# Row tiles 4 to 15 of the input stream loaded by features and normalised by GpSimd and VectorE

## The chip, the cores and the metric

The kernel runs on one core of a Trainium2 chip, as one launch. The metric is the device time of one execution in microseconds (us). Engine names in the profile: PE is TensorE, PEld its weight loads, DVE is VectorE, ACT is ScalarE, POOL is GpSimd, SP is SyncE, which here only issues DMAs.

## The reference, cut to what matters

One transformer-like layer over 256 latent tokens (`x`) and 256 context tokens (`ctx`) of 2048 features, in fp32. Only its opening concerns the change:

```python
shift, scale, gate = split(silu(c) @ w_mod + b_mod, 3)       # and the same from c_ctx
u   = layer_norm(x)   * (1 + scale)   + shift                # mean and variance over the 2048 features
u_c = layer_norm(ctx) * (1 + scale_c) + shift_c
p   = u   @ w_in
p_c = u_c @ w_in[:, :N_KV]
```

Everything behind it (a gated linear recurrence, an attention branch, gates, an output projection) works on `p` and `p_c`.

## The kernel before

The 2048 features are 16 row tiles `kt` of 128. Products want the features on the partitions, so `u` is kept as tiles of 128 features by 2x256 tokens, each split into a high and a low fp32r part; a product is three matmuls, `three` and `three_b` at lines 340 to 348. Weights come as raw fp32 blocks (`raw`, three buffers), are cut into `whi` by ScalarE (L337) and `wlo` by VectorE (L338), two blocks ahead (`LEAD`).

`x` and `ctx` lie in memory with tokens first. `load_rows` (L158) brings them with tokens on the partitions into four tiles `xs`, four row tiles wide each. `ln_stats` (L248) takes mean and variance of each token, so these are one number for each partition, and `normalise` (L258) is one VectorE tensor_scalar with two scalars per partition. `make_x` (L271) normalises four row tiles at a time (8 instructions of 128x512 for row tiles 4 to 11; row tiles 0 to 3 are done by `norm_x` from other places). The tile `xs[3]` has been given back by the time row tiles 12 to 15 are wanted, so `make_x` loads each of them again (L279, 128 partitions x 4 pieces of 512 bytes) into a small rotating buffer (tag T2, 4 buffers) and normalises it with four instructions of 128x128. `make_u` (L284) then transposes the row tile on TensorE, four 128x128 transposes into a PSUM bank (L291); ScalarE applies scale and shift from PSUM (L300) and makes the high part (L302), VectorE the low part (L303).

Scale and shift have to be computed first: the rows of `w_mod` come in 512 KB blocks through a pool of AHEAD = 5 buffers (L187). For row tiles 0 to 3 TensorE multiplies them (L204, 16 blocks), for row tiles 4 to 15 VectorE does (`mod_unit`, L225: two instructions of 128x1024 for each block, four blocks for each row tile). `prep_tasks` (L507) strings these together for one row tile: three units, `make_x`, one unit, `make_u`.

The products over the key and value columns run in the order of VISITS: the chunk, and from which row tile to which, so that products start while later row tiles are being prepared. `weave` and `tick` (L353, L365) put the preparing tasks between the matmuls, evenly by number of matmuls. This order is the one in which the program is written. Each engine's own order is made from it by a scheduler, which may take an instruction earlier that waits for nothing; on the chip each engine then runs its list in order, and so does each queue that issues DMAs.

Of the kernel before, what the change touches and what calls it, by code (L numbers as in the profile page):

```python
# [8 lines left out]
F32 = mybir.dt.float32  # L9
# [3 lines left out]
ALU = mybir.AluOpType  # L13
AX = mybir.AxisListType

P = 128
D = 2048
KT = D // P
# [17 lines left out]
LATE = 13  # L36
GATES = (0,) * 13 + (3, 4, 3, 1, 1, 0, 2, 2)
MOD_PE = 4
AHEAD = 5
DEPTH = 3  # L40
TURN = 5
LEAD = 2
# [8 lines left out]
def block_kernel(ctx: ExitStack, tc: tile.TileContext, a: dict, out: bass.AP):  # L51
    nc = tc.nc
# [12 lines left out]
    def nm(s):  # L65
        uid[0] += 1
        return f"{s}_{uid[0]}"

    def slot(n, dt=F32):
        return big.tile([P, BIG], dt, tag="S8", name=nm(n))  # L70
# [7 lines left out]
    def t2(n):  # L78
        return tp.tile([P, 512], F32, tag="T2", name=nm(n), bufs=4)
# [8 lines left out]
    def aux(n):  # L88
        return ps.tile([P, 512], F32, tag="aux", name=nm(n))
# [3 lines left out]
    def other(n):  # L93

        return (aux if flip[0] else acc)(n)

    mm = nc.tensor.matmul
# [16 lines left out]
    ident = cst[:, C_ID:C_ID + P]  # L114
# [30 lines left out]
    nc.vector.tensor_tensor(c8, c8, sg8, op=ALU.mult)  # L145
    mod_pool = tc.tile_pool(name="mod", bufs=AHEAD)
    mod_open = mod_pool.__enter__()

    def mod_tile():
        if late:  # L150
            return t4("mod")
        return mod_open.tile([P, 1024], F32, tag="mod", name=nm("mod"))

    bst = cp.tile([P, 4, 4, 6], F32, name="bst")
    xg = a["xc"].rearrange("(t p) (g d) -> g p t d", p=P, g=4)
    xs = [slot("xs")[:, :D].rearrange("p (t d) -> p t d", t=4) for _ in range(4)]
# [15 lines left out]
    for r in range(8):  # L172
        pt = aux("scb")
# [10 lines left out]
    def ahead():  # L184
        while stream and len(blocks) < (2 if late else AHEAD):
            t = mod_tile()
            nc.sync.dma_start(t, stream.pop(0))  # L187
            blocks.append(t)
# [47 lines left out]
    def unit_tasks(js, vs):  # L236
        return [(lambda j=j, hf=hf: mod_unit(j, hf, vs), a["w_mod"][j, hf]) for j in js for hf in range(2)]
# [7 lines left out]
    rs0 = cp.tile([P, 4], F32, name="rs0")  # L245
    ag = cp.tile([P, 4, 2], F32, name="ag0")
# [11 lines left out]
    def normalise(x_, t):  # L258
        nc.vector.tensor_scalar(x_, x_, ag[:, t, 0:1], rs0[:, t:t + 1],
                                op0=ALU.subtract, op1=ALU.mult)  # L260
# [3 lines left out]
    def norm_x(kt, n, ts=range(4)):  # L264

        for t in ts:
            normalise(xs[kt // 4][:, t, (kt % 4) * P:(kt % 4 + n) * P], t)

    x_of, normed = {}, {0}

    def make_x(kt):  # L271
        if kt < 12:
            if kt // 4 not in normed:
                normed.add(kt // 4)
                norm_x(kt // 4 * 4, 4)
            xt = xs[kt // 4][:, :, (kt % 4) * P:(kt % 4 + 1) * P]
        else:
            xt = t2("xt")[:, :512].rearrange("p (t d) -> p t d", t=4)
            nc.sync.dma_start(xt, xg[3][:, :, (kt % 4) * P:(kt % 4 + 1) * P])  # L279
            for t in range(4):  # L280
                normalise(xt[:, t, :], t)
        x_of[kt] = xt

    def make_u(kt, seqs=(0, 1)):  # L284
        xt = x_of[kt]
        if kt >= MOD_PE:
            mod_finish(kt, (0, 1))
            mod_finish(16 + kt, (0, 1))
        pt = other("xT")
        for t in (2 * s + i for s in seqs for i in range(2)):  # L290
            nc.tensor.transpose(pt[:, t * P:(t + 1) * P], xt[:, t, :], ident)  # L291
        uf = t2("uf")[:, :512]
        for s in seqs:
            if u[s][kt // 4] is None:
                u[s][kt // 4] = (slot, wslot)[s]("u", F32R)[:, :2048].rearrange(
                    "p (k h t) -> p k h t", k=4, h=2)
            hi = u[s][kt // 4][:, kt % 4, 0, :]
            lo = u[s][kt // 4][:, kt % 4, 1, :]
            f = uf[:, s * 256:(s + 1) * 256]
            nc.scalar.activation(f, pt[:, s * 256:(s + 1) * 256], AF.Identity,  # L300
                                 bias=mv[:, s, kt:kt + 1], scale=mv[:, s, 16 + kt:17 + kt])
            nc.scalar.copy(hi, f)  # L302
            nc.vector.tensor_tensor(lo, f, hi.bitcast(F32), op=ALU.subtract)  # L303
        made.add(kt)


    turn = [0]
# [199 lines left out]
    def prep_tasks(kt):  # L507

        ts = unit_tasks((kt, 16 + kt), (0, 1))
        ts.insert(3, lambda: make_x(kt))  # L510
        return ts + [lambda: make_u(kt)]

    def gate_task(j):
# [3 lines left out]
    for c, k0, k1 in VISITS:  # L517
        _, w, i = chunks[c]
# [9 lines left out]
    between = [[] for _ in VISITS]  # L528
    sums, totals = zip(*(col_tasks(kt) for kt in range(MOD_PE)))
    xu = [(lambda kt=kt: make_x(kt), lambda kt=kt: make_u(kt)) for kt in range(MOD_PE)]  # L530
# [1 line left out]
    tasks.append(totals[0])  # L532
    x_of[0] = xs[0][:, :, 0:P]
    between[1] += sums[1]
    between[2] += [totals[1], xu[1][0], *sums[2][:2], xu[1][1], *sums[2][2:]]
    between[3] += [totals[2], xu[2][0], *sums[3][:1], xu[2][1], *sums[3][1:], lambda: None,
                   totals[3], xu[3][0], lambda: None, xu[3][1]]
    units = [t for kt in range(MOD_PE, KT) for t in prep_tasks(kt)]
# [439 lines left out]
    for c in range(4):  # L978
        i = 8 + (2 * c - 1) * n
# [135 lines left out]
    pt = aux("gr")[:16, :P]  # L1115
# [98 lines left out]
def _swap(w):  # L1214
    return w.reshape(2, 2, 32)[:, ::-1].reshape(HD)


def _layout(i):
    import numpy as np
    w = i["w_in"][0]  # L1220
    cst, rope = _constants()
    qn, kn = i["q_norm_w"][0], i["k_norm_w"][0]
    cw = np.concatenate([i["conv_w"][0], i["conv_b"]], 0)
    xc = np.concatenate([i["x"][0], i["ctx"][0]], 0)
    return {
        "xc": xc,
        "cf": np.stack([i["c"][0], i["c_ctx"]]).reshape(2, KT, P).transpose(2, 1, 0)
        .reshape(P, 32),
        "cc": np.concatenate([i["c"][0], i["c_ctx"]]).reshape(8, 512),
        "w_mod1": i["w_mod"][0].reshape(4, 4, P, 3, KT, P)[:, :, :, :2, :MOD_PE]  # L1230
        .transpose(4, 0, 2, 1, 3, 5).reshape(MOD_PE, 4, P, 1024),
        "w_mod": i["w_mod"][0].T.reshape(48, P, 2, 1024).transpose(0, 2, 1, 3),
        "b_mod": i["b_mod"][0].reshape(48, P).T,
        "w_qa": _blocks(w[:, 0:1024], 512),
        "w_ka": _blocks(w[:, 1024:2048], 512),
        "w_va": _halves(w[:, 2048:4096], 512),
        "w_kv": _halves(w[:, 4096:5152], 352),
        "w_o": _halves(w[:, 5152:7200], 512),
        "w_z": _halves(w[:, 7200:9248], 512),
        "w_qb": _halves(w[:, 9248:11296], 512),  # L1240
        "w_zb": _blocks(w[:, 11296:13344], 512),
        "w_g": _halves(w[:, 13344:17440], 512),
        "w_ba": _halves(i["w_branch_a"][0], 512),
        "w_bb": _halves(i["w_branch_b"][0], 512),
        "w_out": _halves(i["w_out"][0], 512),
        "conv": cw.reshape(4, 16, P).transpose(2, 1, 0),
        "b_if": i["b_if"],
        "mh": i["mh_norm_w"],
        "nw": np.concatenate([qn, _swap(qn), kn, _swap(kn)]).reshape(2, 256),
        "ln": np.concatenate([i["ln_w"], i["ln_b"]], 0),  # L1250
        "cst": cst,
        "rope": rope,
    }
# [18 lines left out]
```

## Time and profile before

| | us |
|---|---|
| median of 3 runs | 1346.44 |
| lowest and highest run | 1344.09, 1348.11 |
| the profiled execution | 1343.62 |
| its span in the trace | 1341.6 |
| TensorE busy in the span | 1296.4 |
| VectorE busy in the span | 976.0 |

The span runs from the first to the last instruction of the program; 2.0 us of the profiled execution lie outside. All times below are counted from the start of the span. A row of the timeline merges neighbouring instructions of one kind: start, time from the first start to the last end, engine, line, operation, output and inputs, shape, count, and in brackets how long the engine had been idle and what ended that. Durations of matmuls overlap, because they are pipelined: their pace is read from start to start.

### The profile page before, as it was taken

The numbers are of one execution on the slowest core, as the hardware profiler recorded it, in microseconds if no ns is written. First come the engines' busy times: TensorE is split into PE (matmuls) and PEld (weight loads), VectorE is DVE, ScalarE is ACT, GpSimd is POOL, SyncE is SP. The second block draws the span as 40 slices with busy tenths as digits, with TensorE's granted clock in tenths as the row PEclk, the third lists the DMA queues.
The fourth block names the chain that finished last, engine by engine and source line by source line (L and its number), as shares of the span: only waits on it lengthen the run. The fifth ranks groups of instructions, "written<-read, shape, count | busy, mean of one in ns | idle before, by whom it ended". The sixth has DMA issues, their size and how long they took to land.

```text
span 1341.6 us, 19662 instructions
## 1 busy us (share of the span) xinstructions
PE 1296.4 (97%) x7541; PEld 1161.7 (87%) x7541; DVE 976.0 (73%) x1577; ACT 649.8 (48%) x928; POOL 54.1 (4%) x83
## 2 busy tenths in 40 slices
PE   6999998999999999999999999999999999999996
PEld 3788988999999988888889999998888888888884
DVE  6698998877986678787787868786555455545667
ACT  4544322324334576676755566565444444434441
POOL 0000000000110011010110000000000000000000
PEclk8999998999999999999999999999999999999999
DMA  9876764885435554555455444445655556576663
GB/s 339 310 260 227 251 221 136 296 306 189 143 111 189 195 167 160 171 181 180 155 162 182 139 161 142 143 139 174 204 198 202 204 197 203 195 275 219 218 219 116
DMA packets 77902, 264.17 MB, mean 197 GB/s; under 512 B 8984, under 2 KB 11688, under 8 KB 77168
## 3 DMA queue, kind: packets, MB, share of 16 engines
q1 hardware_dynamic: 74752, 251.99, 55.5%
q0 software_dynamic: 2448, 10.68, 2.4%
q8 instruction: 59, 0.97, 0.3%
q10 hardware_dynamic: 608, 0.24, 0.1%
q14 instruction: 35, 0.29, 0.1%
HBM read 260.75 MB, written 2.14 MB: 196 GB/s over the span
## 4 chain that ended last, share of the span: by engine, by line
PE 46%; DVE 2%; ACT 1%; DMA 1%; issue 0%; DVEq 0%; ACTq 0%
PE zb L347 2%; PE zb L346 2%; PE zb L348 2%; PE yb L343 2%; PE yb L342 2%; PE yb L341 2%; PE ga L343 2%; PE ga L341 2%; PE ga L342 2%; PE ya L343 2%; PE ya L341 2%; PE ya L342 2%; PE gb L342 2%; PE gb L343 2%; PE gb L341 2%; PE q L342 2%
## 5 line engine op out<-in xcount | busy, mean ns | idle before, releaser
L338 DVE TENSOR_TENSOR wlo<-raw,whi 128x1024 fp32r<-128x1024 f32 (+3 forms) x375 | 445.3, 1190 | 264.5 <-ACT whi L337 259.4
L337 ACT CAST whi<-raw 128x1024 fp32r<-128x1024 f32 (+3 forms) x375 | 380.2, 1016 | 449.2 <-PE p L343 130.8
L342 PE MATMUL p<-wlo,u 128*128 128x512 f32 (+1 forms) x448 | 160.1, 357 | 2.5 <-DVE wlo L338 2.4
L341 PE MATMUL p<-whi,u 128*128 128x512 f32 (+1 forms) x448 | 159.3, 358 | 2.1 <-ACT u L302 1.1
L225 DVE SCALAR_TENSOR_TENSOR junk<-mod,sc 128x1024 bf16<-128x1024 f32 x128 | 153.4, 1221 | 9.4 <-DMA mod<-in_w_mod 9.3
L343 PE MATMUL p<-whi,u 128*128 128x512 f32 (+1 forms) x448 | 159.4, 356 | 0.0
L342 PEld LDWEIGHTS p<-wlo,u 128*128 128x128 f32 x448 | 86.5, 193 | 10.8 <-DVE wlo L338 4.2
L341 PEld LDWEIGHTS p<-whi,u 128*128 128x128 f32 x448 | 85.7, 192 | 11.5 <-ACT u L302 2.5
L343 PEld LDWEIGHTS p<-whi,u 128*128 128x128 f32 x448 | 86.6, 193 | 6.8
L346 PE MATMUL zb<-u,whi 128*128 128x256 f32 x256 | 72.0, 281 | 0.0
L346 PE MATMUL p<-u,whi 128*128 128x256 f32 x256 | 70.6, 278 | 0.7 <-ACT u L302 0.7
L348 PE MATMUL p<-u,wlo 128*128 128x256 f32 x256 | 70.3, 275 | 0.2 <-DVE wlo L338 0.2
L347 PE MATMUL zb<-u,whi 128*128 128x256 f32 x256 | 70.4, 275 | 0.0
L348 PE MATMUL zb<-u,wlo 128*128 128x256 f32 x256 | 70.4, 275 | 0.0
L347 PE MATMUL p<-u,whi 128*128 128x256 f32 x256 | 70.4, 275 | 0.0
L346 PEld LDWEIGHTS p<-u,whi 128*128 128x128 f32 x256 | 48.9, 192 | 2.1 <-ACT u L302 1.2
L341 PE MATMUL z<-whi,u 128*128 128x512 f32 x128 | 49.7, 389 | 0.0
L341 PE MATMUL q<-whi,u 128*128 128x512 f32 x128 | 49.7, 388 | 0.0
L347 PEld LDWEIGHTS p<-u,whi 128*128 128x128 f32 x256 | 49.1, 192 | 0.4 <-issue 0.4
L342 PE MATMUL gb<-wlo,u 128*128 128x512 f32 x128 | 48.7, 381 | 0.8 <-DVE wlo L338 0.8
L342 PE MATMUL z<-wlo,u 128*128 128x512 f32 x128 | 49.2, 384 | 0.2 <-DVE wlo L338 0.2
L348 PEld LDWEIGHTS p<-u,wlo 128*128 128x128 f32 x256 | 49.1, 192 | 0.3 <-DVE wlo L338 0.3
(329 smaller groups left out, 3156.9 us busy)
## 6 DMA issues: line engine op xcount, KB each, us to landing
mod<-in_w_mod SPq DMA_DIRECT2D x96, 512.0 KB, 4.9
raw<-in_w_g SPq DMA_DIRECT2D x64, 512.0 KB, 4.1
raw<-in_w_o SPq DMA_DIRECT2D x32, 512.0 KB, 3.5
raw<-in_w_z SPq DMA_DIRECT2D x32, 512.0 KB, 3.6
raw<-in_w_qb SPq DMA_DIRECT2D x32, 512.0 KB, 3.6
raw<-in_w_zb SPq DMA_DIRECT2D x32, 512.0 KB, 3.4
raw<-in_w_ba SPq DMA_DIRECT2D x32, 512.0 KB, 3.5
raw<-in_w_bb SPq DMA_DIRECT2D x32, 512.0 KB, 4.1
```

The lines of the kernel that those rows point to most:

```text
L225: nc.vector.scalar_tensor_tensor(junk, blk, 1.0, sc[v][:, hf * 1024:(hf + 1) * 1024], op0=ALU.mult, op1=ALU.mult, accum_out=mp[:, v, hf, j ...
L337: nc.scalar.copy(hi, src)
L338: nc.vector.tensor_tensor(lo, src, hi.bitcast(F32), op=ALU.subtract)
L341: mm(o, lhsT=xh, rhs=wh, start=start, stop=False)
L342: mm(o, lhsT=xh, rhs=wl, start=False, stop=False)
L343: mm(o, lhsT=xl, rhs=wh, start=False, stop=stop)
L346: mm(o, lhsT=wh, rhs=xh, start=start, stop=False)
L347: mm(o, lhsT=wh, rhs=xl, start=False, stop=False)
L348: mm(o, lhsT=wl, rhs=xh, start=False, stop=stop)
```

## The change

Row tiles 0 to 3 stay as they are (ROWS = 4). For row tiles 4 to 15 the host hands over a transposed copy `xT`, features first, in blocks of 128 features by 512 tokens (256 KB each). `fetch_x` issues the load of one row tile on SP: row tiles 4 to 11 into the room of `xs[1]` and `xs[2]`, whose tokens-first content was needed for the statistics only; row tiles 12 to 15 into the small rotating buffers. Now the mean and the factor of a token have to be spread along the free axis: `stat_rows`, once, multiplies the broadcast statistics by the identity on TensorE (8 products of 128x128), and ScalarE copies the two PSUM banks to `mr` in SBUF. `make_x` becomes one GpSimd subtraction and one VectorE multiplication of 128x512, and `make_u` has no transposes for these row tiles: ScalarE reads `xt` from SBUF. `mr` takes 4 KB of each partition, as much as one `w_mod` buffer, and AHEAD goes from 5 to 4. `make_x` stands one unit earlier in `prep_tasks`. Row tile 4 is fetched in `stat_rows`, row tiles 5 to 11 each at the end of the `make_u` of the row tile before, row tiles 12 to 15 in `make_x`.

```diff
-AHEAD = 5
+AHEAD = 4
+ROWS = 4
...
+    mr = mod_open.tile([P, 2, 512], F32, name="mr", bufs=1)
...
+    def stat_rows():
+        for i, src in enumerate((ag[:, :, 0], rs0)):
+            pt = other("mr")
+            for t in range(4):
+                mm(pt[:, t * P:(t + 1) * P], lhsT=src[:, t:t + 1].to_broadcast([P, P]), rhs=ident,
+                   start=True, stop=True)
+            nc.scalar.copy(mr[:, i, :], pt)
+        fetch_x(ROWS)
+
+    def fetch_x(kt):
+        if kt < 12:
+            xt = xs[kt // 4].rearrange("p t d -> p (t d)")[:, (kt % 4) * 512:(kt % 4 + 1) * 512]
+        else:
+            xt = t2("xt")[:, :512]
+        nc.sync.dma_start(xt, a["xT"][kt - ROWS])
+        x_of[kt] = xt
 
     def make_x(kt):
-        if kt < 12:
-            if kt // 4 not in normed:
-                normed.add(kt // 4)
-                norm_x(kt // 4 * 4, 4)
-            xt = xs[kt // 4][:, :, (kt % 4) * P:(kt % 4 + 1) * P]
-        else:
-            xt = t2("xt")[:, :512].rearrange("p (t d) -> p t d", t=4)
-            nc.sync.dma_start(xt, xg[3][:, :, (kt % 4) * P:(kt % 4 + 1) * P])
-            for t in range(4):
-                normalise(xt[:, t, :], t)
-        x_of[kt] = xt
+        if kt < ROWS:
+            x_of[kt] = xs[kt // 4][:, :, (kt % 4) * P:(kt % 4 + 1) * P]
+            return
+        if kt not in x_of:
+            fetch_x(kt)
+        xt = x_of[kt]
+        nc.gpsimd.tensor_tensor(xt, xt, mr[:, 0, :], op=ALU.subtract)
+        nc.vector.tensor_tensor(xt, xt, mr[:, 1, :], op=ALU.mult)
...
-        pt = other("xT")
-        for t in (2 * s + i for s in seqs for i in range(2)):
-            nc.tensor.transpose(pt[:, t * P:(t + 1) * P], xt[:, t, :], ident)
+        pt = xt
+        if kt < ROWS:
+            pt = other("xT")
+            for t in (2 * s + i for s in seqs for i in range(2)):
+                nc.tensor.transpose(pt[:, t * P:(t + 1) * P], xt[:, t, :], ident)
...
         made.add(kt)
+        if ROWS <= kt < 11:
+            fetch_x(kt + 1)
...
-        ts.insert(3, lambda: make_x(kt))
+        ts.insert(2, lambda: make_x(kt))
...
-    between[2] += [totals[1], xu[1][0], *sums[2][:2], xu[1][1], *sums[2][2:]]
+    between[2] += [totals[1], xu[1][0], *sums[2][:2], xu[1][1], *sums[2][2:], stat_rows]
...
+        "xT": xc.T.reshape(KT, P, 512)[ROWS:],
```

## Rows read from the trace of the kernel before

**Rows 1.** The page, part 1: busy us, share of the span, instructions.
```profile
PE 1296.4 (97%) x7541; PEld 1161.7 (87%) x7541; DVE 976.0 (73%) x1577; ACT 649.8 (48%) x928; POOL 54.1 (4%) x83
```
**Rows 2.** Busy time by stretch: stretch, length, engines, granted clock, DMA share, GB/s.
```profile
34.00:58.00 24.00, 21.12 (x201) 16.21 (x201) 14.02 (x27) 13.10 (x27) 0.00 (x0) 1.00 0.91 333
58.00:168.00 110.00, 109.56 (x559) 97.63 (x558) 101.81 (x191) 45.37 (x79) 0.15 (x2) 1.00 0.73 246
168.00:201.00 33.00, 32.20 (x153) 27.88 (x152) 32.97 (x64) 8.99 (x14) 0.00 (x0) 1.00 0.70 222
201.00:235.00 34.00, 30.65 (x171) 29.23 (x170) 28.70 (x62) 7.46 (x12) 0.60 (x1) 0.90 0.43 137
235.00:268.00 33.00, 31.85 (x211) 31.02 (x210) 26.48 (x67) 10.82 (x17) 0.00 (x0) 1.00 0.83 297
```
**Rows 3.** Timeline of PE, 57.4 to 59 us: four transposes and the matmuls behind.
```profile
57.50 0.63 PE L291 MATMUL xT<-cst,xs 128*128 128x128 f32 x4
57.89 0.46 PE L341 MATMUL p<-whi,u 128*128 128x512 f32 x1
58.19 0.38 PE L342 MATMUL p<-wlo,u 128*128 128x512 f32 x1
58.41 0.38 PE L343 MATMUL p<-whi,u 128*128 128x512 f32 x1
```
**Rows 4.** One line, L596: fp32 products with 128 columns, the four of `gi`.
```profile
L596 PE MATMUL gi<-cst,gw x8: 272/273/276, 293.0 to 293.8; 128*8 128x128 f32 x8
```
**Rows 5.** Timeline of PE, 47 to 57.9 us: one product of the modulation.
```profile
52.48 0.64 PE L204 MATMUL mod<-mod,cf 128*32 128x256 f32 x8 [0.76 <-DMA mod<-in_w_mod]
```
**Rows 6.** Timeline of SP, the DMA issues, in two stretches.
```profile
44.31 1.15 SPq L187 DMA_DIRECT2D mod<-in_w_mod  x2
...
46.04 4.62 SPq L187 DMA_DIRECT2D mod<-in_w_mod  x4
...
204.56 0.38 SPq L279 DMA_DIRECT2D xt<-in_xc  x1
```
**Rows 7.** DMA issues by line: count, KB each, median us from issue to landing.
```profile
mod<-in_w_mod SPq DMA_DIRECT2D x96, 512.0 KB, 4.9
...
xt<-in_xc SPq DMA_DIRECT2D x4, 256.0 KB, 5.4
```
**Rows 8.** Timeline of POOL from the start: its DMA issue of L565.
```profile
1.31 0.70 POOL L565 DMA_DIRECT2D cst<-in_cst  x1 [0.38 <-issue]
```
**Rows 9.** Groups of DVE by shape, 14 to 33 us and 460 to 620 us.
```profile
L259 DVE TENSOR_SCALAR xs<-xs,ag,rs 128x512 f32<-128x512 f32 x8 | 3.9, 548 | 0.0
...
L883 DVE TENSOR_TENSOR ws<-ws,qT 128x512 f32<-128x512 f32 x5 | 3.4, 686 | 0.0
```
**Rows 10.** Timeline of DVE around row tiles 12 and 14.
```profile
177.28 1.12 DVE L259 TENSOR_SCALAR xt<-xt,ag,rs 128x128 f32<-128x128 f32 x4
178.30 1.23 DVE L338 TENSOR_TENSOR wlo<-raw,whi 128x1024 fp32r<-128x1024 f32 x1
...
210.57 1.12 DVE L259 TENSOR_SCALAR xt<-xt,ag,rs 128x128 f32<-128x128 f32 x4 [1.94 <-DMA xt<-in_xc]
...
212.20 0.89 DVE L338 TENSOR_TENSOR wlo<-raw,whi 128x704 fp32r<-128x704 f32 x1
```
**Rows 11.** Timeline of POOL, 588 to 594 us: two multiplications of 128x512.
```profile
588.74 3.51 POOL L813 TENSOR_TENSOR G<-G,mh 128x512 f32<-128x512 f32 x2 [3.40 <-ACT G L812]
```
**Rows 12.** Timeline of DVE in the same stretch, 588 to 594 us.
```profile
589.63 3.70 DVE L338 TENSOR_TENSOR wlo<-raw,whi 128x1024 fp32r<-128x1024 f32 x2 [0.91 <-ACT whi L337]
```
**Rows 13.** Timeline of PE, 206.9 to 214.3 us, around row tile 14.
```profile
207.98 0.76 PE L341 MATMUL p<-whi,u 128*128 128x352 f32 x4
211.02 1.05 PE L291 MATMUL xT<-cst,xt 128*128 128x128 f32 x4 [2.28 <-DVE xt L259]
213.14 0.66 PE L342 MATMUL p<-wlo,u 128*128 128x352 f32 x1 [1.07 <-DVE wlo L338]
```
**Rows 14.** Busy time by stretch behind that wait, columns as in the second group.
```profile
212.50:219.30 6.80, 6.16 (x21) 6.16 (x22) 5.21 (x12) 0.00 (x0) 0.00 (x0) 0.50 0.33 106
```

More of the change, by code (lines that the diff above doesn't have):

```diff
@@ L267, in norm_x @@
             normalise(xs[kt // 4][:, t, (kt % 4) * P:(kt % 4 + n) * P], t)
-    x_of, normed = {}, {0}
-    def make_x(kt):
-        if kt < 12:
-            if kt // 4 not in normed:
-                normed.add(kt // 4)
-                norm_x(kt // 4 * 4, 4)
-            xt = xs[kt // 4][:, :, (kt % 4) * P:(kt % 4 + 1) * P]
-        else:
-            xt = t2("xt")[:, :512].rearrange("p (t d) -> p t d", t=4)
-            nc.sync.dma_start(xt, xg[3][:, :, (kt % 4) * P:(kt % 4 + 1) * P])
-            for t in range(4):
-                normalise(xt[:, t, :], t)
-        x_of[kt] = xt
+    x_of = {}
+    def stat_rows():
[13 more added lines that the diff above has]
+        x_of[kt] = xt
+    def make_x(kt):
+        if kt < ROWS:
[6 more added lines that the diff above has]
+        nc.vector.tensor_tensor(xt, xt, mr[:, 1, :], op=ALU.mult)
     def make_u(kt, seqs=(0, 1)):
```

## The prediction

> **What bounds the kernel now.** I read the page first, for which engine fills the span; then the busy times by stretch, for what the opening is limited by; then the timelines of single engines at the places the change touches; last the groups of instructions, for prices. The page says TensorE: 97% busy, VectorE 73% [rows 1]. But busy is not pace, and the average hides the opening, which is all the change touches. By stretch it falls into three parts [rows 2]. From 34 to 58 us neither compute engine is full (TensorE 21.1 of 24 us, VectorE 14.0 of 24); there the DMA is at 0.91 of its time, and products wait for `w_mod` blocks: the one at 52.48 had waited 0.76 us for its load [rows 5]. From 58 to 168 us TensorE is full (109.56 of 110) and runs at its pace of 0.22 us from one 512-column matmul to the next [rows 3]; VectorE has 8.2 us left of 110. From 168 to 235 us VectorE is the tight one (32.97 of 33, then 28.70 of 34), TensorE has gaps, and the granted clock falls. The largest gap is at row tile 14: matmuls stop at 208, the transposes wait 2.28 us for the normalised tile, the next matmul waits 1.07 us for a `wlo` [rows 13], and then 6.8 us pass at half clock, 1.2 of 2.4 GHz, with TensorE having just been idle [rows 14]. VectorE had itself stood 1.94 us waiting for the tile's load, with the cut of that `wlo` two places behind [rows 10].
>
> **The change, part by part.** The sum is made against the profiled execution, 1343.6 us, which is 2.8 under the median of the three runs shown, 1346.4. What this measurement can tell from no change is about 0.3%, 4.0 us.
>
> *Transposes.* Four take 0.39 us of TensorE's pace (57.50 to 57.89), and the matmul behind them 0.30 in place of 0.22 [rows 3]. Twelve row tiles lose them: 12 x 0.47 = 5.6 us. Without the slow matmul it would be 12 x 0.39 = 4.7; that is the lower bound. Seven or eight of the twelve lie where TensorE is full, so nothing hides them and the gain is real there, as long as VectorE follows. **-5.6**.
>
> *Statistics along the free axis.* Eight fp32 products of 128 columns. Such a product is two records, and the eight records of `gi` start within 0.8 us, 0.11 apart [rows 4]: 16 x 0.11 = 1.8 us. Cover: TensorE has 2.9 us idle in 34 to 58 [rows 2], but it is idle there because it waits for loads, in order, and the eight come on top. Bounds 0 and 1.8; I take **+1.8**. ScalarE's two copies lie beside other work (13.1 of 24 us busy); so would its reading from SBUF in place of PSUM, which no row prices.
>
> *One `w_mod` buffer less.* A block's load is issued when a buffer comes free. In the busy part of the start the loads leave SP about 1.4 us apart (four within 4.62 us) [rows 6], so each is issued about 1.4 us later; the product at 52.48, already late [rows 5], would be later by that much at worst and not at all where the queue was the limit. Bounds 0 and 1.4, I take the middle: **+0.7**. From 58 to 168 us some eight row tiles are prepared, 14 us each with four blocks, so a block is used every 3.5 us and three blocks ahead are 10 us; landing takes 4.9 [rows 7]: nothing.
>
> *Loads.* Twelve of 256 KB come, four go: 2.1 MB more. At the 333 GB/s of the start that is 6.3 us, if all of it were pushed in front of the `w_mod` blocks. This can happen: the scheduler takes what waits for nothing early, as it took the load of L565, which stands in the program with the gate computations of the middle and was issued at 1.31 us [rows 8]; the eight loads into `xs` wait for the statistics only. From 58 us on the DMA is at 0.73 [rows 2] and has 30 us to spare. Bounds 0 and 6.3; **+0.5**, because from 34 to 58 us the blocks wait for buffers as well as for the queue, and because a row tile early is one that nobody waits for later.
>
> *VectorE's own instructions.* Away: eight of 128x512, together 3.9 us [rows 9], and four groups of 1.12 us for row tiles 12 to 15 [rows 10], 4.5. New: twelve products of 128x512 at 0.69 [rows 9], 8.2. The balance is -0.2: **0**. Where it falls changes: 3.9 us leave the start, up to 5.5 come where VectorE is fuller.
>
> *GpSimd's subtractions.* GpSimd is free (0.15 us busy of 110 [rows 2]). Two multiplications of this size took it 3.51 us, 1.75 each, beside a busy VectorE [rows 11]. They are not free for VectorE: the two cuts it made meanwhile took 3.70 us [rows 12], where one alone takes 1.23 [rows 10], so 1.24 us were lost, 0.62 to each of GpSimd's. Twelve cost VectorE 0 to 7.4 us. The first eight can run early, where VectorE has 10 of 24 us idle. The last four fall in 168 to 235 us: 2.5 us, of which 5.3 us of idle time [rows 2] hides about half: **+1.2**.
> The Trainium skill (GPSIMD Engine Reference, section 8, Key points) says that GpSimd shares its SBUF interfaces with VectorE and contends with VectorE instructions that have two SBUF inputs; the trace agrees, with the 3.70 us above. The page gives no price; if every subtraction shut VectorE out for its whole length the loss would be, as an estimate with the row's 1.75 us, 21 us in place of 7.4, and the row speaks for the smaller.
>
> *New waits.* VectorE's multiplication now waits for GpSimd, which waits for the load. Queued behind it on VectorE are the cuts `wlo` and the modulation units, and TensorE waits for the cuts. For row tiles 4 to 11 the load is out a row tile ahead, those 14 us. For 12 to 15 the load is issued as before and lands after 5.4 us [rows 7]; `make_x` stands one unit earlier, which gives two units, 2 x 2.4 us of VectorE, between it and `make_u`. On SP each added load is one more issue of 0.38 us [rows 6], and SP is idle most of the time. ScalarE's scale and shift, which waited for the transposes, now waits for the multiplication; `whi` copies stand behind it, as before. I take the waits as **0**, with the stall at row tile 14 as it is: TensorE no longer stops at a transpose, but VectorE still stops, and the same `wlo` is behind it.
>
> Sum: -5.6 + 1.8 + 0.7 + 0.5 + 1.2 = -1.4 us, so 1342.2 against the profiled execution and **1345.0** against the median.
>
> **The rivals.**
> *A, the stall at row tile 14 goes.* The wait of 2.28 us was one of the transposes, which are gone, and 1.07 and half of the 6.8 us at half clock came after it: 2.28 + 1.07 + 3.4 = 6.8 us [rows 13, 14]. For it: TensorE has other matmuls to do, and the tile itself is needed much later; and of the four row tiles loaded like this only one stalled, by the accident of where a change of chunk fell. Against it: VectorE's order, which this rival needs changed. 1345.0 - 6.8 = 1338.2.
> *B, VectorE stands behind GpSimd.* Place: row tiles 12 to 15, 168 to 235 us, where VectorE has 0.03 and 5.3 us idle. The tile that was ready at landing is ready 1.75 us later [rows 11]: four times, 7.0 us, and with 2.5 us of contention 9.5, more than the idle 5.3. It decides from the point at which the waits exceed what is idle, that is from three late tiles on. Then TensorE waits for `wlo`, and another stretch at half clock like the one above costs 3.4 us: +7.0 + 3.4, so 1355.4. For it: rows 12 and the 1.94 us that VectorE already waited [rows 10]. Against it: the earlier place of `make_x`.
> *C, the start takes it.* Place: the `w_mod` blocks before 58 us. If the scheduler puts the eight loads in front of them, the 6.3 us come in place of 0.5 and the 1.4 in place of 0.7: +6.5, so 1351.5. It decides from the point at which more than the idle 0.09 x 24 = 2.2 us of DMA are added, that is from three early loads on. Against it: SP's order of issue puts most blocks ahead.
> *D, the transposes were hidden anyway,* because VectorE limits 58 to 168 us as soon as TensorE is faster: its 8.2 idle us shrink by the 5.6 gained. Then -5.6 falls away: 1350.6.
>
> **How the numbers follow.** Forecast 0.36, A 0.35, B 0.18, C 0.08, D 0.03. The likeliest is the forecast, 1345, with a range of its own of 1342 to 1350 (the loads and GpSimd's contention towards their upper ends, the statistics hidden at the lower). Faster by over 0.3% is A: 0.35. Within 0.3% is the forecast: 0.36. Slower is B, C and D, which all lie beyond 4.0 us: 0.29. For 8 in 10 the range goes through A down to 1334 (the stall gone, the statistics and half of the start's costs hidden too) and up through B's middle to 1357; about 0.1 is left out on each side.
>
> **What the profile after would show.** Transposes: 16 left of 64, and each row tile's 14 us becoming 0.5 shorter in 58 to 168 us. Statistics: 16 records of 128 columns before 58 us. Buffers and loads: products L204 that wait for `w_mod` for longer than 0.76 us, and come later than it. GpSimd: twelve subtractions of about 1.75 us, with VectorE's instructions beside them stretched. B would show VectorE idle in front of the multiplication, released by GpSimd, and TensorE behind it waiting for `wlo` in 168 to 235 us; A would show that stretch at full clock. The prediction is wrong if the stretch from 168 to 235 us changes by more than 5 us, or if what stands at 58 us is moved by more than 4.

## The result: 0.6% slower, and the profile after

| | before | after |
|---|---|---|
| median of 7 runs each, us | 1344.09 | 1350.93 |
| lowest and highest run | 1338.55, 1348.11 | 1350.09, 1353.89 |
| the profiled execution (its span) | 1343.62 (1341.6) | 1353.89 (1352.1) |
| ratio to before, 95% interval | | 1.0062 [1.0044, 1.0080] |

The forecast was a small gain, 1345.0 against 1346.4. The change costs 0.6%, 7 us between the medians and 8 by the ratio; the time lies inside the range, on the other side of no change. The profiled execution of after is 3 us above its median.

The difference is made before the gate computations. Their first product (`gc`, L596 before, L619 after) starts 6.65 us later, against 6.84 us between the medians. The two spans differ by 10.5 us, but what lies behind this product took 1063.6 to 1069.7 us in three traces of the kernel before and its variants alone, so the other 3.9 us are within what single executions differ by. Timeline of PE, before and then after (start, duration, engine, line):

```profile
275.85 0.39 PE L596 MATMUL gc<-tri,gw 128*8 128x128 f32 x2
```
```profile
282.50 0.39 PE L619 MATMUL gc<-tri,gw 128*8 128x128 f32 x2
```

Busy time by stretch of after, to be laid beside [rows 2] (length, PE, PEld, DVE, ACT, POOL, granted clock, DMA share, GB/s):

```profile
34.00:58.00 24.00, 22.66 (x206) 17.36 (x198) 12.29 (x22) 14.18 (x31) 1.66 (x5) 1.00 0.86 303
58.00:168.00 110.00, 100.22 (x485) 86.56 (x485) 109.23 (x194) 43.22 (x75) 12.39 (x9) 0.97 0.76 252
201.00:235.00 34.00, 30.26 (x164) 26.84 (x162) 34.00 (x58) 9.83 (x16) 3.33 (x2) 1.00 0.55 180
```

From 58 to 168 us the roles have changed places: before, TensorE was full and VectorE had 8.2 us left; now VectorE is full (109.23 of 110) and TensorE has 9.8 us of gaps. From 201 to 235 us VectorE has no gap at all. The half clock behind row tile 14 [rows 14] is gone: the stretch from 201 to 235 us runs at 1.00.

How far TensorE gets in 58 to 168 us is read from its groups of 512-column products (line, operation, shape, count, busy us, mean ns, idle before). Before, then after:

```profile
L341 PE MATMUL p<-whi,u 128*128 128x512 f32 x137 | 52.3, 383 | 0.0
L342 PE MATMUL p<-wlo,u 128*128 128x512 f32 x136 | 51.8, 381 | 0.4 <-DVE wlo L338 0.4
L343 PE MATMUL p<-whi,u 128*128 128x512 f32 x136 | 51.5, 379 | 0.0
```
```profile
L365 PE MATMUL p<-wlo,u 128*128 128x512 f32 x116 | 45.8, 394 | 5.5 <-DVE wlo L361 5.5
L364 PE MATMUL p<-whi,u 128*128 128x512 f32 x117 | 45.6, 390 | 1.9 <-ACT u L323 1.9
L366 PE MATMUL p<-whi,u 128*128 128x512 f32 x116 | 45.6, 393 | 0.4 <-DVE u L324 0.4
```

409 products before, 349 after: 60 x 0.22 us [rows 3] = 13.2 us behind at 168 us, 2.2 of it brought from the start (the first such product stands at 60.09 in place of 57.89). Behind 168 us after gets about half back, to 6.65, nearly all of it at row tile 14 (table in the section on the prediction's steps). The wait that is new is the one for `wlo`, VectorE's cut of the weights: 0.4 us before, 5.5 (with the 352-column products 6.0) after.

What was added to VectorE's work stands in two timelines side by side. GpSimd's subtractions (L300), and VectorE's instructions at the same times:

```profile
84.54 1.57 POOL L300 TENSOR_TENSOR xs<-xs,mr 128x512 f32<-128x512 f32 x1 [14.30 <-DMA xs<-in_xT]
87.66 1.29 POOL L300 TENSOR_TENSOR xs<-xs,mr 128x512 f32<-128x512 f32 x1 [1.54 <-DMA xs<-in_xT]
101.36 4.43 POOL L300 TENSOR_TENSOR xs<-xs,mr 128x512 f32<-128x512 f32 x2 [6.76 <-DMA xs<-in_xT]
```
```profile
83.75 1.22 DVE L361 TENSOR_TENSOR wlo<-raw,whi 128x1024 fp32r<-128x1024 f32 x1
84.89 2.30 DVE L227 SCALAR_TENSOR_TENSOR junk<-mod,sc 128x1024 bf16<-128x1024 f32 x1
87.73 2.30 DVE L227 SCALAR_TENSOR_TENSOR junk<-mod,sc 128x1024 bf16<-128x1024 f32 x1
...
102.34 2.30 DVE L361 TENSOR_TENSOR wlo<-raw,whi 128x1024 fp32r<-128x1024 f32 x1
104.56 2.30 DVE L227 SCALAR_TENSOR_TENSOR junk<-mod,sc 128x1024 bf16<-128x1024 f32 x1
```

Beside each of these four subtractions one VectorE instruction takes 2.30 us in place of 1.22: 1.08 us more, for a product of the modulation (L227) as for a cut (L361). Of all twelve, ten cost VectorE 1.08 us each, one 0.84, and one nothing, as VectorE stood waiting for its result: 11.6 us.

The rows show how. The two engines take turns. The subtraction of 84.54 ends at 86.11, 1.14 us after the VectorE instruction that was running when it began (83.75 + 1.22 = 84.97). VectorE's next instruction ends 1.08 us after the subtraction (84.89 + 2.30 = 87.19). So it is at all of the lengthened instructions of this size. GpSimd's own rows, 1.27 to 2.27 us, contain its wait for VectorE.

Seven of the twelve subtractions lie in 58 to 168 us. VectorE's multiplications (L301) are there too; its groups in that stretch:

```profile
L227 DVE SCALAR_TENSOR_TENSOR junk<-mod,sc 128x1024 bf16<-128x1024 f32 x60 | 76.6, 1306 | 0.1
...
L301 DVE TENSOR_TENSOR xs<-xs,mr 128x512 f32<-128x512 f32 x7 | 4.7, 677 | 0.0
```

So 7 x 1.08 + 4.7 = 12.3 us were put into a stretch where VectorE had 8.2. This sum is an argument, not a measurement: the experiments show that GpSimd's part of it costs and the multiplications don't.

They lie there because the loads do. Timeline of SP, issues of row tiles 4, 5, 6 and the last of the eight:

```profile
48.82 0.43 SPq L290 DMA_DIRECT2D xs<-in_xT  x1
...
62.46 0.42 SPq L290 DMA_DIRECT2D xs<-in_xT  x1
...
77.53 0.41 SPq L290 DMA_DIRECT2D xs<-in_xT  x1
...
101.68 0.42 SPq L290 DMA_DIRECT2D xs<-in_xT  x1
```

The loads were not taken early to the start: one leaves before 58 us, the others in the order of the program up to 101.68, and each subtraction shown follows its landing.

VectorE's delay costs TensorE more than the waits. Timeline of PE in after:

```profile
112.58 0.48 PE L365 MATMUL p<-wlo,u 128*128 128x512 f32 x1 [2.44 <-DVE wlo L361]
...
117.08 0.48 PE L364 MATMUL p<-whi,u 128*128 128x512 f32 x1 [1.87 <-ACT u L323]
...
119.41 0.63 PE L366 MATMUL p<-whi,u 128*128 128x512 f32 x1
119.84 0.63 PE L364 MATMUL p<-whi,u 128*128 128x512 f32 x1
```

After gaps of 2.44 and 1.87 us the products start 0.43 us apart in place of 0.22, at the lower of the two clocks, for some 3 us; the mean clock of 0.97 in the stretch above is this and a like piece at 61 to 64 us. The second piece is not the subtractions' doing: the run without them, below, has one too (mean clock 0.98).

### The profile page after: what moved, and what is told of

It reads as the page before. It is cut to its first block, busy times and chain, and to the rows that moved or that the text cites. A ratio compares the mean times of both kernels' runs of the same rounds, so it can differ in the third digit from the quotient of the medians.

```text
span 1352.1 us, 19610 instructions
## 1 busy us (share of the span) xinstructions
PE 1295.4 (96%) x7509; PEld 1156.3 (86%) x7509; DVE 985.0 (73%) x1565; ACT 651.4 (48%) x930; POOL 74.9 (6%) x95
## 5 line engine op out<-in xcount | busy, mean ns | idle before, releaser
L361 DVE TENSOR_TENSOR wlo<-raw,whi 128x1024 fp32r<-128x1024 f32 (+3 forms) x375 | 447.7, 1197 | 256.2 <-ACT whi L360 255.8
L227 DVE SCALAR_TENSOR_TENSOR junk<-mod,sc 128x1024 bf16<-128x1024 f32 x128 | 160.5, 1276 | 13.6 <-DMA mod<-in_w_mod 13.4
L364 PE MATMUL ga<-whi,u 128*128 128x512 f32 x128 | 49.4, 386 | 0.0
```

The lines of the kernel that those rows point to most:

```text
L227: nc.vector.scalar_tensor_tensor(junk, blk, 1.0, sc[v][:, hf * 1024:(hf + 1) * 1024], op0=ALU.mult, op1=ALU.mult, accum_out=mp[:, v, hf, j ...
L361: nc.vector.tensor_tensor(lo, src, hi.bitcast(F32), op=ALU.subtract)
L364: mm(o, lhsT=xh, rhs=wh, start=start, stop=False)
```

## The experiments

All times are ratios to runs of the kernel before on the same chip, with the 95% interval in brackets; 0.001 is 1.34 us. Theory 1: GpSimd's subtractions lengthen VectorE's instructions, and VectorE becomes the limit of the opening. Theory 2: the multiplications that VectorE itself got suffice for that. Theory 3: the missing `w_mod` buffer delays the start, and all behind it.

### The buffer alone (theory 3)

The kernel before with one buffer less:

```diff
-AHEAD = 5
+AHEAD = 4
```

> The kernel before with four w_mod buffers in place of five, nothing else. Theory 1 (each GpSimd subtraction shuts VectorE out for 1.08 us, in the stretch from 58 to 168 us where VectorE has 8.2 us idle): no more than 1 us, ratio 0.999 to 1.001. Theory 2 (VectorE's own multiplications, moved from the start into that stretch, are enough): the same. Theory 3 (the missing buffer delays the start): most of the 7 us, ratio 1.003 to 1.005, and the stretch from 34 to 58 us longer.

Measured 1.0012 [0.9986, 1.0037]. The first 512-column product starts at 58.81 in place of 57.89, and the first gate product at 275.40, not later than before. The interval alone still reaches theory 3's 1.003; but all runs of the change below have four buffers too, and one of them is faster than before. Theory 3 is out as the main cause.

### The subtraction on VectorE (theory 2)

The changed kernel without GpSimd:

```diff
-        nc.gpsimd.tensor_tensor(xt, xt, mr[:, 0, :], op=ALU.subtract)
+        nc.vector.tensor_tensor(xt, xt, mr[:, 0, :], op=ALU.subtract)
```

> The changed kernel with the subtraction on VectorE too. VectorE pays 0.6 us for it in place of the 1.08 us that GpSimd's keeps it out. Theory 1: 12 x 0.48 = 5.8 us less VectorE time, so faster than the changed kernel by 2 to 5 us, ratio to before 1.002 to 1.005, and no instruction of 128x1024 over 1.3 us. Theory 2: VectorE has still more of its own, 12 x 0.6 = 7 us, ratio 1.008 to 1.011. Theory 3: no change, 1.006.

Measured 0.9996 [0.9984, 1.0008]. VectorE got twelve more instructions of its own, 12 x 0.69 = 8.2 us, and the kernel is 0.0066, 8.9 us, faster than after. Theory 1 had expected less, 2 to 5 us: VectorE's account is 11.6 - 8.2 = 3.4 us, and 1.2 us for which it had waited for GpSimd. TensorE's mean clock in the stretch below, 1.00 against 0.97, is worth about 3 us more, as an estimate (0.03 of 110 us); no run separates these. The stretch 58 to 168 us:

```profile
58.00:168.00 110.00, 104.86 (x518) 91.40 (x517) 109.83 (x208) 45.60 (x80) 0.15 (x2) 1.00 0.80 267
```

VectorE is as full as in after (109.83), but gets through 208 instructions in place of 194, and TensorE through 518 in place of 485. That busy time is full in both shows that it can't tell the two apart; the counts can. Theory 2 falls.

### No subtraction, and neither subtraction nor multiplication

The changed kernel with the GpSimd line left out, and with both lines left out:

```diff
-        nc.gpsimd.tensor_tensor(xt, xt, mr[:, 0, :], op=ALU.subtract)
```
```diff
-        nc.gpsimd.tensor_tensor(xt, xt, mr[:, 0, :], op=ALU.subtract)
-        nc.vector.tensor_tensor(xt, xt, mr[:, 1, :], op=ALU.mult)
```

> The changed kernel without the subtraction of the mean, so this step of the normalisation is missing. Theory 1: VectorE gets 12 x 1.08 = 13 us back, 7.6 of them from 58 to 168 us, and the kernel is as fast as before or faster, ratio 0.995 to 1.000. Theory 2: the multiplications alone keep it slow, 1.003 to 1.006. Theory 3: no change, 1.006.

> The changed kernel with neither the subtraction nor the multiplication: row tiles 4 to 15 are not normalised. Left are the new loads, the statistics, four w_mod buffers and the missing transposes. Theory 1a (VectorE bounds 58 to 168 us in every form of the change, so each us of its own work counts as much as a us that GpSimd keeps it out): 12 x 0.6 us less than without the subtraction alone, 0.991 to 0.995. Theory 1b (only what GpSimd takes matters; with it gone TensorE bounds again): as without the subtraction, 0.996 to 0.998.

Without the subtraction: 0.9968 [0.9955, 0.9980], 0.0094 or 12.6 us below after, for the 11.6 us by which VectorE's instructions had been lengthened and the 1.2 us of its wait. The first gate product moves from 282.50 to 270.32, 12.2 us. Without both: 0.9984 [0.9971, 0.9998], no further gain: the multiplications, 8.2 us, cost nothing that can be measured, and theory 1a's larger gain of leaving them out didn't come. (The subtractions on VectorE, 8.2 us too, cost 0.0028 or 3.7 us against none.) So a us of VectorE's own work in the opening counts for less than a us of its waiting for GpSimd; why was not settled. Even with neither VectorE is busy for 109.70 of 110 us. The stretch 58 to 168 us without the subtraction, then two stretches without both:

```profile
58.00:168.00 110.00, 106.05 (x521) 93.12 (x518) 109.86 (x208) 45.52 (x79) 0.15 (x2) 0.98 0.83 274
```
```profile
58.00:168.00 110.00, 104.70 (x524) 91.70 (x525) 109.70 (x207) 46.08 (x80) 0.15 (x2) 1.00 0.84 283
201.00:235.00 34.00, 33.80 (x207) 32.35 (x207) 22.09 (x40) 9.80 (x18) 0.60 (x1) 1.00 0.60 196
```

VectorE has 22.09 of 34 us busy in the later stretch (28.70 in [rows 2]): it does in 58 to 168 us what it did later before. From 58 to 168 us TensorE still waits for `wlo` three times, 3.8 us together. Why it has just these gaps wasn't settled.

### The subtractions without the change

The kernel before, with four buffers, and with twelve GpSimd subtractions of 128x512 that read a `w_mod` block and write to a scratch tile that nobody reads:

```diff
+        if MOD_PE <= j < 16 and hf == 1:
+            nc.gpsimd.tensor_tensor(scr[:, 0, :], blk[:, 0:512], scr[:, 1, :], op=ALU.subtract)
```

> The kernel before with four w_mod buffers and twelve GpSimd subtractions of 128x512 whose result nobody needs, one for each row tile from 4 to 15, on a w_mod block. Loads, transposes and VectorE's work are those of before. Theory 1: twelve VectorE instructions beside them take 1.08 us longer; in 58 to 168 us this is 8 x 1.08 = 8.6 us against 8.2 us idle, so 1 to 6 us slower, ratio 1.001 to 1.005. Theory 2: no change against the kernel before with four buffers. Theory 3: what that kernel shows and no more.

Measured 1.0040 [1.0025, 1.0055], first gate product at 281.31 in place of 275.85. None of the change's waits, loads or statistics are there; instructions on an otherwise idle engine, whose results nobody uses, cost 5.4 us, or 3.8 against the run with the buffer alone. This second difference, 0.0028, is just not clear of the noise (about 0.003 either way); by the traces the first gate product is 5.9 us later. They do hold a block's buffer a little longer. The run agrees with theory 1 without the change around it, but not with its place: VectorE's instructions get 8.6 us longer in 58 to 168 us, of which TensorE loses 1.4 us there and 1.9 us more up to 206.

### The subtraction twice, and a second instruction with one input

```diff
         nc.gpsimd.tensor_tensor(xt, xt, mr[:, 0, :], op=ALU.subtract)
+        nc.gpsimd.tensor_tensor(xt, xt, mr[:, 0, :], op=ALU.subtract)
```
```diff
         nc.gpsimd.tensor_tensor(xt, xt, mr[:, 0, :], op=ALU.subtract)
+        nc.gpsimd.tensor_scalar(xt, xt, 0.0, None, op0=ALU.add)
```

> The changed kernel with every GpSimd subtraction done twice, so that the mean is taken off twice and 24 of them run in place of 12. Theory 1 (each one makes one VectorE instruction 1.08 us longer, and VectorE is the limit of the opening): 12 x 1.08 = 13 us more of VectorE, of which 8 to 13 us reach the end: 1.012 to 1.016 of the kernel before. Rival (the changed kernel loses by the chain from load over GpSimd to VectorE, that is by a tile that is ready later): the tiles are loaded a row tile ahead and wait anyway, another 1.5 us is hidden: 1.005 to 1.008, like the changed kernel.

> The changed kernel with a second GpSimd instruction behind each subtraction, one that reads one tensor only (adds the constant 0.0). If VectorE is shut out by any GpSimd instruction of this size, the time is that of the run with the subtraction twice, 1.012 to 1.016. If it is shut out only where GpSimd reads two tensors, VectorE's instructions beside the additions keep their 1.22 us and the time is the changed kernel's, 1.005 to 1.008.

Twice: 1.0143 [1.0115, 1.0171], 0.0081 or 10.9 us above after. VectorE's instructions get 22.1 us longer, 10.5 more than in after, and it waits for GpSimd for 3.7 us in place of 1.2. The time is theory 1's; a chain that hides the second subtraction is out. The stretch 58 to 168 us has VectorE full with fewer instructions again, 182, and the mean clock is down to 0.92:

```profile
58.00:168.00 110.00, 98.86 (x451) 84.99 (x452) 109.64 (x182) 39.04 (x68) 26.69 (x16) 0.92 0.72 234
```

One input: 1.0129 [1.0094, 1.0163]. By the time alone this is the first of the two expectations, that any GpSimd instruction shuts VectorE out alike. The trace says otherwise. Timeline of GpSimd (L301 here is the addition), then of VectorE:

```profile
103.22 1.48 POOL L300 TENSOR_TENSOR xs<-xs,mr 128x512 f32<-128x512 f32 x1 [3.06 <-DMA xs<-in_xT]
104.79 1.54 POOL L301 TENSOR_SCALAR xs<-xs 128x512 f32<-128x512 f32 x1
106.30 1.36 POOL L300 TENSOR_TENSOR xs<-xs,mr 128x512 f32<-128x512 f32 x1
107.75 2.34 POOL L301 TENSOR_SCALAR xs<-xs 128x512 f32<-128x512 f32 x1
```
```profile
96.98 1.23 DVE L233 TENSOR_TENSOR mv<-mp 128x2 f32<-128x2 f32 x1
98.14 0.68 DVE L302 TENSOR_TENSOR xs<-xs,mr 128x512 f32<-128x512 f32 x1
98.74 0.56 DVE L235 TENSOR_TENSOR mv<-mv,bm 128x2 f32<-128x2 f32 x1
99.22 0.15 DVE L233 TENSOR_TENSOR mv<-mp 128x2 f32<-128x2 f32 x1
100.19 0.69 DVE L302 TENSOR_TENSOR xs<-xs,mr 128x512 f32<-128x512 f32 x1 [0.83 <-POOL xs L301]
...
104.91 1.62 DVE L227 SCALAR_TENSOR_TENSOR junk<-mod,sc 128x1024 bf16<-128x1024 f32 x1
...
106.46 2.28 DVE L227 SCALAR_TENSOR_TENSOR junk<-mod,sc 128x1024 bf16<-128x1024 f32 x1
...
108.67 1.62 DVE L362 TENSOR_TENSOR wlo<-raw,whi 128x1024 fp32r<-128x1024 f32 x1
```

Beside a subtraction 1.22 becomes 2.28 to 2.30, beside an addition 1.62: 0.40 us for one input, 1.08 for two. What is added is the same for every length: an instruction of 128x2, 0.15 us, becomes 1.23 beside a subtraction and 0.56 beside an addition. Ten of the twelve additions met a VectorE instruction, 4.0 us; the subtractions cost 10.3 in place of 11.6, as two met VectorE waiting (one in after) and two in part (one in after). This is 2.7 us more of VectorE than in after, but the time grew by 9.0 (1.0129 less 1.0062). The rest fits the other wait that the longer chain on GpSimd made: VectorE waited for GpSimd 0.8 us before 168 us, as the row at 100.19 shows, and 5.8 us in three waits behind it, against 1.2 us in after. That sum, 2.7 + 6.6 - 1.2 = 8.1, is near the 9.0, but no run separates the two; the chain rival, which the run with two subtractions spoke against, has the larger part here.

### Which of the subtractions cost

```diff
-        nc.gpsimd.tensor_tensor(xt, xt, mr[:, 0, :], op=ALU.subtract)
+        (nc.vector if kt < 12 else nc.gpsimd).tensor_tensor(xt, xt, mr[:, 0, :], op=ALU.subtract)
```

and the counterpart with the two engines exchanged.

> The changed kernel with the subtraction on VectorE for row tiles 4 to 11 and on GpSimd for 12 to 15 only. Theory 1 with its place in 58 to 168 us: the seven of after that fell there are gone, so 7 x 1.08 = 7.6 us come back and 8 subtractions of 0.69 us come onto VectorE: close to all on VectorE, 0.999 to 1.003. If the place that costs is 168 to 235 us, as the forecast's rival B had it, nothing comes back: 1.004 to 1.008.

> The counterpart: subtraction on GpSimd for row tiles 4 to 11, on VectorE for 12 to 15. Theory 1 with its place in 58 to 168 us: the loss stays, 1.003 to 1.007. If the place that costs is 168 to 235 us: 0.998 to 1.002.

GpSimd for the last four only: 1.0011 [0.9988, 1.0033]. For the first eight only: 1.0021 [1.0005, 1.0038]. The second is less than was expected: neither place alone makes the loss of after. With the products counted as above, and the first gate product:

| subtraction on GpSimd | 512-column products in 58 to 168 us | first gate product, us | ratio |
|---|---|---|---|
| none (all on VectorE) | 388 | 274.61 | 0.9996 |
| row tiles 12 to 15 | 386 | 275.85 | 1.0011 |
| row tiles 4 to 11 | 352 | 277.21 | 1.0021 |
| all (after) | 349 | 282.50 | 1.0062 |

The first eight cost 36 products, 7.9 us, by 168 us; but if the last four are not on GpSimd, most of it is regained behind 201 us. Part of that is a wait of 2.09 us for a `wlo` at 214 us in the run that it is compared with, all on VectorE. With all twelve on GpSimd less is regained. That VectorE has time there for the one and not for the other is the likely reason, but not shown. The stretch 201 to 235 us, of the last four only and then of the first eight only:

```profile
201.00:235.00 34.00, 33.20 (x194) 31.25 (x193) 33.65 (x64) 10.52 (x19) 4.66 (x3) 1.00 0.58 176
```
```profile
201.00:235.00 34.00, 33.18 (x190) 31.00 (x190) 33.55 (x63) 8.60 (x14) 0.27 (x1) 1.00 0.54 168
```

TensorE gets 194 and 190 products done there, in after 164. The intervals of the two ratios overlap, so the traces, one of each, carry this more than the times do.

### Other places for the work

The new way for row tiles 12 to 15 only (`ROWS = 12`, the rest as before); all eight loads with the statistics ahead of the first products; and, with the subtraction on VectorE, the modulation of row tile 4 given from VectorE to TensorE (`MOD_PE = 5`):

```diff
-ROWS = 4
+ROWS = 12
```
```diff
-        fetch_x(ROWS)
+        for kt in range(ROWS, 12):
+            fetch_x(kt)
...
-    between[2] += [totals[1], xu[1][0], *sums[2][:2], xu[1][1], *sums[2][2:], stat_rows]
+    between[2] += [totals[1], xu[1][0], *sums[2][:2], xu[1][1], *sums[2][2:]]
...
+    stat_rows()
```
```diff
-MOD_PE = 4
+MOD_PE = 5
...
+    between[4] += [*sums[4], totals[4], xu[4][0], lambda: None, xu[4][1]]
```

> The changed kernel with ROWS = 12: only row tiles 12 to 15 go the new way, 4 to 11 are normalised at the start and transposed as before. From 58 to 168 us no GpSimd subtraction is left. Theory 1: that stretch is as in the kernel before, and four subtractions of 1.08 us fall in 168 to 235 us, where VectorE was full to 168 to 201 us only: ratio 0.999 to 1.003. A theory that puts the loss on the statistics or on the missing buffer: 1.004 to 1.006.

> The changed kernel with the statistics spread and all eight loads of row tiles 4 to 11 issued before the first products, so that GpSimd can subtract where VectorE is idle. Theory 1: from 58 to 168 us VectorE's long instructions are gone and TensorE gains 5 to 8 us there; but the eight loads and the multiplications, which VectorE's list has ahead of the cuts, hold up the start by 4 to 12 us: ratio 0.998 to 1.006, with the start of the 512-column matmuls later by that much. If place doesn't matter, 1.006 as the changed kernel with no change at the start.

> The changed kernel with the subtraction on VectorE and the modulation of row tile 4 moved from VectorE to TensorE: VectorE loses eight instructions of 1.22 us, 9.8 us, TensorE gets sixteen products more, 2.3 us. Theory 1 (VectorE bounds 58 to 168 us): faster than with the subtraction on VectorE alone by 4 to 8 us, ratio to before 0.994 to 0.997. If TensorE bounds there: slower by 2, 1.001 to 1.003.

The last four only: 1.0022 [1.0009, 1.0034]. The start loses 3.4 us (61.3 in place of 57.9 for the first 512-column product), and only 0.6 of it is regained by the first gate product: at row tile 14 TensorE waits 3.62 us for a `wlo`, and the stretch 201 to 235 us is at a mean clock of 0.90 again.

All eight early: 1.0030 [1.0018, 1.0043], less than after. This is the place that the prediction had in mind:

```profile
34.00:58.00 24.00, 17.34 (x142) 14.14 (x139) 18.42 (x25) 7.59 (x20) 8.64 (x9) 0.86 0.63 232
```

The subtractions are here now (GpSimd 8.64 us), and from the first 512-column product to the gates it is 212.0 us in place of 222.4 in after; up to the 409th product it loses 1.3 us against before, where after loses 11.0. But the first product stands at 65.8: 7.9 us later than before, TensorE has only 17.34 of 24 us busy. The early place has a price too.

Row tile 4 on TensorE: 1.0039 [1.0019, 1.0059], a miss; a gain was expected. Its stretches:

```profile
58.00:66.00 8.00, 6.30 (x36) 3.99 (x36) 7.61 (x15) 3.25 (x9) 0.00 (x0) 0.79 0.86 296
66.00:74.00 8.00, 8.00 (x52) 5.23 (x51) 5.19 (x9) 1.73 (x5) 0.00 (x0) 1.00 0.97 356
```

VectorE is freed from 66 us on (5.19 of 8 us), but before that TensorE waits 2.0 us for one of its blocks and runs at a mean clock of 0.79, and then the DMA is at 0.97 of its time. TensorE has 360 of the 512-column products done by 168 us in place of 388.

No kernel that computes the whole was faster than before.

## Why the prediction was wrong, by its steps

**The step that failed is GpSimd's subtractions, +1.2 us.** Measured: 8.9 us against doing them on VectorE, 12.6 us against leaving them out. It failed twice.
- *Price.* 0.62 us each, against 1.08. The two cuts of [rows 12] had lost 1.24 us, and this was shared out between the two GpSimd multiplications of [rows 11]. One by one, the same rows of before say something else. GpSimd, then VectorE:

```profile
588.74 1.29 POOL L813 TENSOR_TENSOR G<-G,mh 128x512 f32<-128x512 f32 x1 [3.40 <-ACT G L812]
590.17 2.08 POOL L813 TENSOR_TENSOR G<-G,mh 128x512 f32<-128x512 f32 x1
```
```profile
589.63 1.48 DVE L338 TENSOR_TENSOR wlo<-raw,whi 128x1024 fp32r<-128x1024 f32 x1 [0.91 <-ACT whi L337]
591.06 2.27 DVE L338 TENSOR_TENSOR wlo<-raw,whi 128x1024 fp32r<-128x1024 f32 x1
```

  The first multiplication ran for the most part while VectorE was idle, and cost the first cut 0.25 us. The second met VectorE at work and cost 1.04, near the 1.08 of after. The 1.75 us of the estimate "for its whole length" were too long, since the 2.08 contain GpSimd's wait for the first cut; its idea, that VectorE waits until GpSimd has done, was right. The cost to VectorE, 11.6 us, is outside the bounds of 0 to 7.4 and below the 21.
- *Place.* The first eight were to run in 34 to 58 us. One did, at 52.90. The premise was the load of [rows 8], which the scheduler had taken early; these loads it issued in program order. So seven fell into the stretch that the prediction itself had found with 8.2 us of VectorE left, with 4.7 us of multiplications beside them. The prediction says that up to 5.5 us come "where VectorE is fuller", and then books the balance of the whole kernel, zero, in place of that of the stretch. By the stretch's balance either alone would have fitted into 8.2 us and the sum, 12.3, would not; a warning, though not a measure, as the multiplications turned out to cost nothing.

**The rest of the sum came near by luck.** Without that term it is -5.6 + 1.8 + 0.7 + 0.5 = -2.6 us. The run without the subtraction gives 0.9968, -4.3 us [-6.0, -2.7]. But the gain is not where the sum has it. The table has by how much later than before TensorE begins the same product (minus: earlier):

| us | 1st product of 512 columns | 241st | 409th | in front of row tile 14 | behind it | first gate product |
|---|---|---|---|---|---|---|
| before, at | 57.9 | 111.7 | 168.0 | 206.2 | 221.0 | 275.8 |
| after | 2.2 | 13.0 | 13.2 | 14.2 | 7.8 | 6.6 |
| all on VectorE | 1.5 | 3.8 | 4.5 | 3.3 | -0.3 | -1.2 |
| no subtraction | 1.7 | 3.1 | 4.3 | 3.4 | -3.8 | -5.5 |
| before, with subtractions | 1.8 | 2.9 | 3.3 | 5.2 | 5.0 | 5.5 |

The two products about row tile 14, before and then without the subtraction:

```profile
206.19 0.31 PE L341 MATMUL p<-whi,u 128*128 128x352 f32 x1
...
221.03 0.31 PE L341 MATMUL p<-whi,u 128*128 128x352 f32 x1
```
```profile
209.56 0.31 PE L363 MATMUL p<-whi,u 128*128 128x352 f32 x1
...
217.19 0.31 PE L363 MATMUL p<-whi,u 128*128 128x352 f32 x1
```

- *Start.* +1.8, +0.7 and +0.5 were booked; the first 512-column product is 2.2 us later, 1.7 without the subtraction. With one buffer less alone it is 0.9 later. The rate from 34 to 58 us fell (303 GB/s, 333 before [rows 2]), and only one of the new loads is issued there (48.82): they crowded little out.
- *Transposes, -5.6.* This step failed too. From the first 512-column product to the first gate product it is 218.0 us before and 210.8 without the subtraction, -7.2 us; but up to row tile 14 nothing of it has come, TensorE is 1.7 us further behind there than at its start. What the transposes give is used up by new gaps: TensorE is idle for 4.0 us of 58 to 168 us without the subtraction (106.05 busy of 110), 0.4 before.
- *The stall at row tile 14, left as it is.* Here the gain was made: 7.2 us without the subtraction, 6.4 in after, 3.7 with all on VectorE, 0.2 in the kernel before with subtractions. Two errors, the transposes and the stall, offset each other. Why the stall goes wasn't settled; in the run with the last four only it stayed.
- *VectorE's own instructions, 0.* Right by the run without the multiplications, which is not faster than the one with them.
- *New waits, 0.* VectorE waited for GpSimd once in the opening, for 1.2 us: close. TensorE's new waits for VectorE were left out, see the transposes.

**The rivals.** A: the stall at row tile 14 did go, with its half clock [rows 13, 14]; after regains 6.4 us there, and A was priced at 6.8. A was right in its place and price; the kernel is slower all the same, by what was lost before. B had the pair of engines right, and its condition, that GpSimd takes more than VectorE has idle; but it looked at 168 to 235 us alone and at VectorE waiting for GpSimd's results. The larger loss was made before 168 us, and it was VectorE's instructions getting longer. D had the place, 58 to 168 us, and that the gain of the transposes falls away there; it reckoned VectorE's idle time to shrink by what TensorE gained, not by what VectorE was given. Against the 1346.4 that the prediction started from, B came to +9.0 us and C to +5.1, and measured were +6.8 to +8.3; but C's cause, loads in front of the blocks, is not in the trace.

The prediction named as its own refutation a change of the start by over 4 us or of the stretch from 168 us on by over 5. The second sign did come, but as a gain: from 168 us to the gates TensorE regains 6.6 us. The prediction left out the stretch between, where the loss was made: TensorE's work there was priced step by step, VectorE's only in rival D, at a chance of 0.03.

## What to carry to other kernels

An idle GpSimd is no free engine beside a busy VectorE: price each of its instructions as VectorE time, here 1.08 us for a two-input one of 128x512, more than the 0.69 us for which VectorE does the same itself. Read such a price from a single pair of rows in which both engines were at work, not from a mean. Book moved work by the stretch in which it will run, not by the kernel's balance, and take the place of a load from the program's order unless the trace shows that kind of load being taken early. Where an engine is full in both of two versions, compare the counts of instructions it got through, and the progress of the engine behind it, not its busy share. When a total comes out near the sum, follow the same instruction through both traces before the single terms are believed.

## What the runs showed of the hardware

- A GpSimd subtraction of 128x512 in fp32 adds 1.08 us to one VectorE instruction with two SBUF inputs, a GpSimd addition of a constant 0.40 us, and the amount is the same for an instruction of 0.15 us as for one of 1.22. GpSimd's own instruction shows 1.27 to 2.35 us, because its wait for VectorE is part of it: GpSimd's subtraction ends 1.14 us after VectorE's instruction before it, and VectorE's next one, of 128x1024, 1.08 us after that (rows at 83.75 to 84.89). The Trainium skill (SBUF — State Buffer, Summary: rules for kernel authors) says that of a VectorE instruction with two SBUF inputs and a GpSimd instruction that reads SBUF the second one to issue is blocked until the first has finished. For the subtraction the traces agree, in both directions. For the addition they don't: VectorE's instruction beside it is 0.40 us longer and ends 0.20 us after it (104.91 + 1.62 against 104.79 + 1.54), so the two overlap.
- In after, TensorE ran at the lower clock for some 3 us at 118 us, having stood still for 2.44, 1.87 and 0.43 us shortly before; with the subtractions doubled the mean clock of 58 to 168 us is 0.92. Part of what a late `wlo` or `u` costs is this.
